# Attention by pairs of heads, in an order enforced on TensorE

## The chip, the cores and the metric

The kernel runs on one core of a Trainium2 chip. The metric is device time in microseconds (us) of one execution. TensorE (PE) multiplies, VectorE (DVE), ScalarE (ACT) and GpSimd (POOL) do the rest, SyncE (SP) issues the DMA transfers. PE's results go to PSUM, the other data to SBUF.

## The reference

Two transformer layers with adaptive norms (adaLN), for 512 tokens and 256 context tokens of width 1024, in float32. Three kinds of attention matter here; the rest (projections, SwiGLU feed-forward, norms, pooling) is outside the change.

```python
# layer 0: 12 query heads, 4 key/value heads, width 64; main queries see 768 keys, context queries 256
attn   = block_attention(q,  concat([kc, k]), concat([vc, v]), scale)
attn_c = block_attention(qc, kc, vc, scale)
# layer 1: 8 latent heads (key width 96, 768 keys) ...
o_mla  = block_attention(mq, concat([mkc, mk]), concat([mvc, mv]), mla_scale)
# ... and 8 neighbourhood heads: a window of the grid with a bias, and the 256 context keys
s = concat([s_win * scale + bias, s_ctx * scale]); p = softmax(s)
o_na = p[window] @ v_w + p[ctx] @ v_ctx
# block_attention: s = q k^T * scale; p = softmax(s); o = p v
```

## The kernel before

The two layers run one after the other: input norm and projection, attention, output projection (`mix_out`), feed-forward. Activations lie with channels in partitions and tokens in columns. Matmuls of float32 data are made of two or three passes: a value is split into a high and a low part of type fp32r (`QH`, `QL`; `KA` and its low part `LA`), and `mm3` (L143 to L145) or the pairs L786/L787, L813/L814, L1084/L1085 add them up.

Attention works on units. In layer 0 a unit is one head (of a pair of heads, `hd` 0 or 1) and one tile of 128 queries: 6 pairs x 4 tiles x 2 heads (`main_units`), then the context queries with 6 pairs x 2 tiles, both heads in one unit (`ctx_units`). In layer 1 come the neighbourhood units (`na_units`: 4 pairs x 4 blocks, both heads in a unit, 512 keys) and later the latent units (`mla_units`: 4 pairs x 4 tiles x 2 heads). A unit has three steps:

- `scores`: queries x keys on PE into PSUM, then `softmax` (L374 to L387): the maximum on DVE (L378), a small multiply (L380), the exponential with its sum on ACT (L383), the reciprocal on DVE (L385), the scaling on POOL (L387).
- `turn`: the 128 x 128 tiles of the probabilities are transposed on PE (`transposed`, L394) in blocks of three or four into one bank of PSUM, and a block is copied to SBUF (tile `PT`) by ACT (L173) or DVE (L175) in turn.
- the products of values: `V` x `PT`, 64 output channels of a head. The two heads of a pair write partitions 0 to 63 and 64 to 127 of one PSUM tile (L766, L1053, L1235). They are float32, and the trace shows two rows for each.

`pipeline` sets the order of these in the program: scores of unit i, a little background work, then the transposes of unit i - lag (lag 3, 2 and 2 units: `LAG`). The products are background too: `turn` of a pair's second head puts its products into the queue `pvq` in small steps (two key tiles, both heads), and each unit takes 1.4 to 1.8 steps out of it. The other background is `adaq` in layer 0 (16 steps of 8 matmuls of 32 output columns for adaLN weights, L213, each with its DMA loads, and two finishing steps) and `moreq` in latent attention (keys and values of the last four heads, with their transposes, L1129). Only the background has a fixed place (`tc.issue_after(s_().ins)`); else the scheduler of the framework orders each engine's instructions by its own simulated times, and engines run their own list in order.

## Time and profile before

| | us |
|---|---|
| median of three runs (lowest, highest) | 1768.34 (1766.82, 1770.72) |
| the profiled execution, and its span | 1769.58, 1767.8 |
| attention of layer 0, main queries (window 177 to 331): PE busy | 151.83 of 154 |
| neighbourhood attention (1115 to 1184): PE busy | 64.43 of 69 |
| latent attention (1226 to 1346): PE busy | 117.67 of 120 |

A row of the view in order of time is a run of equal instructions on one engine: start, busy time, engine, line, operation, what is written and read, shape, count, and in brackets the idle time before it and who ended it. A matmul's busy time reaches into the next one's, because matmuls are pipelined: from start to start is what a row costs. A row of the view of groups has the busy time in total and the mean of one, then idle time before it.

### The profile page before, as it was taken

What the parts mean: (1) busy time and instruction counts of PE and PEld (TensorE: products, weight loads), DVE (VectorE), ACT (ScalarE), POOL (GpSimd) and SP (SyncE); (2) the same over time, 40 slices, a digit from 0 to 9 for tenths busy, and PEclk for the clock granted to TensorE, in tenths of its full rate; (3) what the DMA queues carried; (4) which work ended last, traced back from release to release, by engine and by line L of the source; (5) the groups of instructions that cost most, each with busy time, mean ns of one, the idle gap of its engine ahead of it and who ended that gap; (6) DMA issues with size and microseconds to landing.
All of it is one profiled execution on the core that took longest, in us unless ns stands there. A gap on an engine that the chain in (4) does not pass through costs nothing.

```text
span 1767.8 us, 29063 instructions
## 1 busy us (share of the span) xinstructions
PE 1702.0 (96%) x11590; PEld 1489.2 (84%) x11590; DVE 946.7 (54%) x2072; ACT 634.5 (36%) x1237; POOL 252.8 (14%) x440
## 2 busy tenths in 40 slices
PE   6898999999999999999999999797999999999999
PEld 3687677788888888888889999677878999899897
DVE  5687565556855534533326875558756543333332
ACT  4454444635221221221124543445545332232231
POOL 1341333302000000000000202455321100000000
PEclk9899999999999999999999999898999999999999
DMA  7401323321534423522122222502003032222221
GB/s 270 159 34 52 119 96 133 130 96 49 187 126 151 169 77 115 175 86 71 61 72 85 84 76 60 127 19 70 30 19 132 13 120 96 96 96 96 95 76 57
DMA packets 60662, 171.23 MB, mean 97 GB/s; under 512 B 7152, under 2 KB 14576, under 8 KB 60528
## 3 DMA queue, kind: packets, MB, share of 16 engines
q1 hardware_dynamic: 60528, 169.39, 28.6%
q8 instruction: 91, 1.49, 0.3%
q14 instruction: 43, 0.35, 0.1%
HBM read 160.05 MB, written 4.19 MB: 93 GB/s over the span
## 4 chain that ended last, share of the span: by engine, by line
PE 92%; DVE 4%; ACT 1%; DMA 1%; issue 1%; SPq 0%; POOL 0%; ACTq 0%; DVEq 0%
PE ps_one L144 17%; PE ps_one L143 17%; PE ps_one L145 17%; PE ps_tp L394 5%; PE ps_tp L145 5%; PE ps_tp L143 5%; PE ps_tp L144 5%; PE ps_pv L766 3%; PE ps_pv L1235 2%; PE ps_big L143 2%; PE ps_big L144 2%; PE ps_big L145 2%; PE ps_pv L1053 1%; PE ps_pv L143 1%; PE ps_pv L144 1%; PE ps_pv L145 1%
## 5 line engine op out<-in xcount | busy, mean ns | idle before, releaser
L131 ACT CAST wH<-wraw 128x1024 fp32r<-128x1024 f32 (+5 forms) x209 | 194.3, 937 | 384.4 <-PE ps_one L144 188.3
L132 DVE TENSOR_TENSOR wL<-wraw,wH 128x1024 fp32r<-128x1024 f32 (+4 forms) x199 | 222.9, 1124 | 167.6 <-ACT wH L131 165.1
L145 PE MATMUL ps_one<-hH,wL 128*128 128x512 f32 (+1 forms) x704 | 236.8, 336 | 0.0
L144 PE MATMUL ps_one<-hL,wH 128*128 128x512 f32 (+1 forms) x704 | 236.8, 336 | 0.0
L143 PE MATMUL ps_one<-hH,wH 128*128 128x512 f32 (+1 forms) x704 | 236.8, 336 | 0.0
L145 PE MATMUL ps_tp<-hH,wL 128*128 128x256 f32 x704 | 196.6, 280 | 0.0
L144 PE MATMUL ps_tp<-hL,wH 128*128 128x256 f32 x704 | 196.3, 280 | 0.0
L143 PE MATMUL ps_tp<-hH,wH 128*128 128x256 f32 x704 | 196.1, 280 | 0.0
L145 PE MATMUL ps_one<-aH,wL 128*128 128x512 f32 (+1 forms) x560 | 194.1, 347 | 0.0
L144 PE MATMUL ps_one<-aL,wH 128*128 128x512 f32 (+1 forms) x560 | 194.0, 347 | 0.0
L143 PE MATMUL ps_one<-aH,wH 128*128 128x512 f32 (+1 forms) x560 | 193.5, 347 | 0.0
L297 POOL TENSOR_SCALAR hH<-nt 128x256 fp32r<-128x256 f32 (+1 forms) x72 | 39.5, 556 | 743.4 <-ACT nt L296 741.4
L145 PEld LDWEIGHTS ps_one<-hH,wL 128*128 128x128 f32 x704 | 132.3, 188 | 15.4
L144 PEld LDWEIGHTS ps_one<-hL,wH 128*128 128x128 f32 x704 | 132.3, 188 | 14.4
L143 PEld LDWEIGHTS ps_one<-hH,wH 128*128 128x128 f32 x704 | 132.3, 188 | 14.1
L387 POOL TENSOR_SCALAR prob<-prob,rs 128x768 f32<-128x768 f32 (+2 forms) x136 | 105.9, 782 | 229.6 <-DVE rs L385 89.1
L143 PEld LDWEIGHTS ps_tp<-hH,wH 128*128 128x128 f32 x704 | 132.4, 189 | 0.9
L144 PEld LDWEIGHTS ps_tp<-hL,wH 128*128 128x128 f32 x704 | 132.1, 188 | 1.0
L145 PEld LDWEIGHTS ps_tp<-hH,wL 128*128 128x128 f32 x704 | 132.3, 188 | 0.1
L143 PEld LDWEIGHTS ps_one<-aH,wH 128*128 128x128 f32 x560 | 105.8, 189 | 14.6
L144 PEld LDWEIGHTS ps_one<-aL,wH 128*128 128x128 f32 x560 | 105.7, 189 | 14.5
L145 PEld LDWEIGHTS ps_one<-aH,wL 128*128 128x128 f32 x560 | 105.6, 189 | 14.5
(300 smaller groups left out, 3567.0 us busy)
## 6 DMA issues: line engine op xcount, KB each, us to landing
wraw<-in_ada_dram SPq DMA_DIRECT2D x80, 512.0 KB, 3.9
wraw<-in_wg_dram SPq DMA_DIRECT2D x44, 512.0 KB, 3.6
wraw<-in_wu_dram SPq DMA_DIRECT2D x44, 512.0 KB, 3.5
wraw<-in_wd_dram SPq DMA_DIRECT2D x32, 384.0 KB, 3.0
wraw<-in_wd_dram SPq DMA_DIRECT2D x16, 512.0 KB, 3.5
wraw<-in_w1n_dram SPq DMA_DIRECT2D x12, 512.0 KB, 3.5
adaw<-in_adaq_dram SPq DMA_DIRECT2D x16, 256.0 KB, 5.4
wraw<-in_adaq_dram SPq DMA_DIRECT2D x8, 512.0 KB, 5.9
```

The source lines that it names most:

```text
L131: act.copy(H, raw[:, :cols])
L132: eng.tensor_tensor(L, raw[:, :cols], H.bitcast(F32), op=ALU.subtract)
L143: pe.matmul(o, aH, bH, start=first, stop=False)
L144: pe.matmul(o, aH, bL, start=False, stop=False)
L145: return pe.matmul(o, aL, bH, start=False, stop=last)
L297: last = (pool.tensor_scalar(H, t[:, :n], 1.0, 1.0, op0=ALU.mult, op1=ALU.mult), sub(L, t[:, :n], H))
L387: pool.tensor_scalar(pr[i], pr[i], r[:, i:i + 1], 1.0, op0=ALU.mult, op1=ALU.mult)
L394: pe.transpose(tp[:, 128 * i:128 * i + 128], b, ident)
L766: pe.matmul(st["pv"][64 * hd:64 * hd + 64, tq], V[kt][:, 64 * kv:64 * kv + 64], pts[hd][:, kt - k0, :], start=kt == k0, stop=kt == 5)
L1053: pe.matmul(o, v[:, hc], pts[hd][:, 2 * (1 - i) + j, :], start=i == 0 and j == 0, stop=i == 1 and j == 1)
L1235: pe.matmul(st["pv"][64 * hd:64 * hd + 64, tq], mV[kt][:, 64 * h:64 * h + 64], pts[hd][:, kt, :], start=kt == 0, stop=kt == 5)
```

## The change

`pipeline` is replaced by `paired`. A unit is now a pair of heads and a query tile (in the context part a pair and both tiles), and the order on PE is fixed: scores of pair i, the first two blocks of transposes of pair i-1, all products of pair i-2, one dose of background, the remaining blocks of transposes of pair i-1. Every block is tied to the last PE instruction issued before it (`Products` remembers it, `block` uses it). Products of the two heads alternate key tile by key tile. The transposes of a layer-0 or latent pair come in three blocks of four tiles (before: two blocks of three for each head), into one `PT` tile of twelve. The background rates are given per pair: `adaq` 0.8 (was 0.35 per unit), `moreq` 1.6 (was 0.8 per unit). Through `Products`, every PE row of the changed kernel carries L45 (matmul) or L49 (transpose).

```diff
-MPVR = 1.4
-PVR0 = 1.4
-PT0 = 6
-WS1, NAPT, MLPT = 4, 6, 5
-LAG = 3, 2, 2
+WS1, NAPT = 4, 6
+class Products:
+    def __init__(self, engine):
+        self.engine, self.last = engine, None
+    def matmul(self, *a, **kw):
+        self.last = self.engine.matmul(*a, **kw)
+        return self.last
+    def transpose(self, *a, **kw):
+        self.last = self.engine.transpose(*a, **kw)
+        return self.last
-    act, dve, pool, pe, sp = nc.scalar, nc.vector, nc.gpsimd, nc.tensor, nc.sync
+    act, dve, pool, pe, sp = nc.scalar, nc.vector, nc.gpsimd, Products(nc.tensor), nc.sync
-    def pipeline(units, fill, lag):
-        pend = []
+    def paired(units, fill):
         debt = [0.0] * len(fill)
+        def block(f):
+            with tc.issue_after(pe.last.ins):
+                f()
         def background():
             for i, (q, rate) in enumerate(fill):
                 debt[i] += rate
                 while debt[i] >= 1.0 and q:
                     debt[i] -= 1.0
-                    q.pop(0)()
+                    block(q.pop(0))
                 if not q:
                     debt[i] = min(debt[i], 1.0)
-        for s_, t_ in units:
-            with tc.issue_after(s_().ins):
-                background()
-            pend.append(t_)
-            if len(pend) > lag:
-                pend.pop(0)()
-        for t_ in pend:
+        units = iter(units)
+        turned = valued = None
+        while True:
+            unit = next(units, None)
+            if unit is None and turned is None and valued is None:
+                break
+            if unit:
+                block(unit[0])
+            for f in turned[1][:2] if turned else ():
+                block(f)
+            if valued:
+                block(valued[2])
             background()
-            t_()
+            for f in turned[1][2:] if turned else ():
+                block(f)
+            unit, turned, valued = None, unit, turned
-        def pv_steps(p, t, last, k0, pts, st, m):
...
+        def values_of(p, t, last, k0, pt, st, m):
             tq = slice(128 * t, 128 * t + 128)
-            def step(k1):
...
+            if t == 0:
+                st["pv"] = ps_pv([P, 512])
+            for kt in range(k0, 6):
                 for hd in range(2):
                     kv = p // 3 + 2 * hd
-                    for kt in (k1, k1 + 1):
-                        pe.matmul(st["pv"][64 * hd:64 * hd + 64, tq], V[kt][:, 64 * kv:64 * kv + 64], pts[hd][:, kt - k0, :],
-                                  start=kt == k0, stop=kt == 5)
...
+                    pe.matmul(st["pv"][64 * hd:64 * hd + 64, tq], V[kt][:, 64 * kv:64 * kv + 64], pt[:, hd, kt - k0, :],
+                              start=kt == k0, stop=kt == 5)
+            if t == last:
+                put_pair(st["pv"], 128 * last + 128, m)
         def main_units(p):
...
+                def turn(i, st=st):
+                    if i == 0:
+                        st["t"] = ap.tile([P, 12, 128], F32, tag="PT", name="PT", bufs=2)
+                    transposed([st["p"][j // 6][:, 0, 128 * (j % 6):128 * (j % 6) + 128] for j in range(4 * i, 4 * i + 4)],
+                               st["t"][:, 4 * i:4 * i + 4, :])
+                def values(t=t, st=st):
+                    values_of(p, t, 3, 0, st["t"].rearrange("p (h k) q -> p h k q", h=2), pvs, mixs[0][2 + p])
+                yield scores, [lambda i=i, turn=turn: turn(i) for i in range(3)], values
...
-        pipeline(all_units(), [(pvq, PVR0), (adaq, 0.35)], LAG[0])
-        for f in adaq + pvq:
+        paired(all_units(), [(adaq, 0.8)])
+        for f in adaq:
             f()
...
-        pipeline((u for pr in range(4) for u in na_units(pr)), [(pvq, 1.8)], LAG[1])
+        paired((u for pr in range(4) for u in na_units(pr)), [])
...
-        pipeline((u for pr in range(4) for u in mla_units(pr)), [(pvq, MPVR), (moreq, MKR)], LAG[2])
+        paired((u for pr in range(4) for u in mla_units(pr)), [(moreq, 2 * MKR)])
```

The neighbourhood, latent and context units are rewritten in the same manner; there the buffers of `prob` become 5 (as before), 4 (was 3) and 4 (as before), and the low queries of the neighbourhood part move to a memory pool of their own (`atq`).

The order that results on PE, in three places. First, layer 0's main queries; KA, QA belong to the first head of a pair, KB, QB to the second, LA and LBm, LBc are the low parts of the keys, and the numbers tell tiles apart. Before:

```order
L766 MATMUL ps_pv_1954<-PT_1902,V4_129 64x128
L766 MATMUL ps_pv_1954<-PT_1902,V5_130 64x128
L766 MATMUL ps_pv_1954<-PT_1928,V4_129 64x128
L766 MATMUL ps_pv_1954<-PT_1928,V5_130 64x128
L786 MATMUL ps_big_2012<-KB0_346,QB_651 128x512
L787 MATMUL ps_big_2012<-LBm_1815,QB_651 128x512
L786 MATMUL ps_big_2012<-KB0_346,QB_651 128x256
L787 MATMUL ps_big_2012<-LBc_1816,QB_651 128x256
L394 MATMUL ps_tp_2002<-ident_76,prob_1892 128x128 x3
L766 MATMUL ps_pv_1954<-PT_1971,V0_125 64x128
L766 MATMUL ps_pv_1954<-PT_1971,V1_126 64x128
L394 MATMUL ps_tp_2007<-ident_76,prob_1892 128x128 x3
```

After:

```order
L49 MATMUL ps_tp_2093<-ident_76,prob_1991 128x128 x4
L49 MATMUL ps_tp_2099<-ident_76,prob_1991 128x128 x2
L49 MATMUL ps_tp_2099<-ident_76,prob_1992 128x128 x2
L45 MATMUL ps_pv_1964<-PT_2021,V0_125 64x128 x2
L45 MATMUL ps_pv_1964<-PT_2021,V1_126 64x128 x2
L45 MATMUL ps_pv_1964<-PT_2021,V2_127 64x128 x2
L45 MATMUL ps_pv_1964<-PT_2021,V3_128 64x128 x2
L45 MATMUL ps_pv_1964<-PT_2021,V4_129 64x128 x2
L45 MATMUL ps_pv_1964<-PT_2021,V5_130 64x128 x2
L45 MATMUL ps_pv_1906<-wraw_2117,cs_112 32x512 x2
L45 MATMUL ps_pv_1906<-wraw_2119,cs_112 32x512 x2
L49 MATMUL ps_tp_2125<-ident_76,prob_1992 128x128 x4
```

Before, one score block of a head stands between two small blocks of products, and two key tiles of one head stand between transposes. After, both heads' scores, eight transposes and twelve products (two trace rows each) follow each other, the heads in alternation; one background step (the two rows of wraw) and the last four transposes close the iteration.

Second, neighbourhood attention, the same engine. Before:

```order
L394 MATMUL ps_tp_11801<-ident_76,prob_11606 128x128 x4
L1053 MATMUL ps_pv_11702<-PT_11707,mV4_9272 64x128
L1053 MATMUL ps_pv_11702<-PT_11707,mV5_9273 64x128
L394 MATMUL ps_tp_11807<-ident_76,prob_11607 128x128 x4
L1053 MATMUL ps_pv_11702<-PT_11708,mV4_9272 64x128
L1053 MATMUL ps_pv_11702<-PT_11708,mV5_9273 64x128
L1053 MATMUL ps_pv_11702<-PT_11707,V20_11021 64x128
L1053 MATMUL ps_pv_11702<-PT_11707,V21_11022 64x128
L1053 MATMUL ps_pv_11702<-PT_11708,V20_11021 64x128
L1053 MATMUL ps_pv_11702<-PT_11708,V21_11022 64x128
```

After:

```order
L49 MATMUL ps_tp_11093<-ident_76,prob_11009 128x128 x4
L49 MATMUL ps_tp_11099<-ident_76,prob_11010 128x128 x4
L45 MATMUL ps_pv_11105<-PT_11043,mV4_9194 64x128
L45 MATMUL ps_pv_11105<-PT_11044,mV4_9194 64x128
L45 MATMUL ps_pv_11105<-PT_11043,mV5_9195 64x128
L45 MATMUL ps_pv_11105<-PT_11044,mV5_9195 64x128
L45 MATMUL ps_pv_11105<-PT_11043,mV0_9190 64x128
L45 MATMUL ps_pv_11105<-PT_11044,mV0_9190 64x128
L45 MATMUL ps_pv_11105<-PT_11043,mV1_9191 64x128
L45 MATMUL ps_pv_11105<-PT_11044,mV1_9191 64x128
L45 MATMUL ps_one_11116<-nKA_9228,nQH0_9220 128x256
```

The products of the unit two back, which stood in pieces between transposes, are one piece behind both blocks of transposes of the unit one back.

Third, the start of latent attention on PE; qr are query tiles with their norms, mKH and mQH the high parts of keys and queries. Before:

```order
L1129 MATMUL ps_tp_12478<-ident_76,qr_12375 96x128 x4
L1129 MATMUL ps_tp_12491<-ident_76,qr_12375 96x128 x4
L143 MATMUL ps_big_12701<-mKH_12075,mQH_12067 128x512
L144 MATMUL ps_big_12701<-mKL_12076,mQH_12067 128x512
L145 MATMUL ps_big_12701<-mKH_12075,mQL_12068 128x512
L143 MATMUL ps_big_12701<-mKH_12075,mQH_12067 128x256
L144 MATMUL ps_big_12701<-mKL_12076,mQH_12067 128x256
L145 MATMUL ps_big_12701<-mKH_12075,mQL_12068 128x256
L1129 MATMUL ps_tp_12619<-ident_76,qr_12540 96x128
L1129 MATMUL ps_tp_12632<-ident_76,qr_12540 96x128
L1129 MATMUL ps_tp_12619<-ident_76,qr_12540 96x128 x3
L1129 MATMUL ps_tp_12632<-ident_76,qr_12540 96x128 x3
```

After:

```order
L49 MATMUL ps_tp_12404<-ident_76,qr_12301 96x128 x4
L49 MATMUL ps_tp_12417<-ident_76,qr_12301 96x128 x4
L49 MATMUL ps_tp_12545<-ident_76,qr_12466 96x128
L49 MATMUL ps_tp_12558<-ident_76,qr_12466 96x128
L49 MATMUL ps_tp_12545<-ident_76,qr_12466 96x128 x3
L49 MATMUL ps_tp_12558<-ident_76,qr_12466 96x128 x3
L49 MATMUL ps_tp_12573<-ident_76,qr_12516 96x128
L49 MATMUL ps_tp_12586<-ident_76,qr_12516 96x128
L49 MATMUL ps_tp_12573<-ident_76,qr_12516 96x128 x3
L49 MATMUL ps_tp_12586<-ident_76,qr_12516 96x128 x3
L45 MATMUL ps_big_12629<-mKH_12001,mQH_11993 128x512
L45 MATMUL ps_big_12629<-mKL_12002,mQH_11993 128x512
```

The first scores stood ahead of the transposes of the last query tiles, and now stand behind all of them.

## Rows read from the trace of the kernel before

**Rows 1.** Stages: window, length, then busy us of each engine, PEclk, DMA.

```profile
177.00:331.00 154.00, 151.83 (x1241) 108.26 (x1242) 93.14 (x239) 80.16 (x187) 49.54 (x62) 0.98 0.37 134
...
1115.00:1184.00 69.00, 64.43 (x524) 52.95 (x524) 41.81 (x178) 39.00 (x94) 34.15 (x73) 0.94 0.26 67
1226.00:1346.00 120.00, 117.67 (x890) 94.10 (x890) 76.13 (x206) 58.78 (x130) 34.74 (x48) 0.98 0.06 19
```

**Rows 2.** The values products alone (L766, L1053, L1235): busy us and count.

```profile
177.00:331.00 154.00, 52.60 (x576) 35.95 (x576) 0.98 0.37 134
...
1115.00:1184.00 69.00, 27.45 (x256) 19.25 (x256) 0.94 0.26 67
...
1226.00:1346.00 120.00, 40.44 (x384) 27.12 (x384) 0.98 0.06 19
```

**Rows 3.** PE in time, 243 to 250 us: start, us, line, operands, count.

```profile
243.07 0.66 PE L766 MATMUL ps_pv<-PT,V 128*64 128x128 f32 x8
...
244.29 0.47 PE L786 MATMUL ps_big<-KA,QA 128*128 128x512 f32 x1
...
244.84 0.28 PE L786 MATMUL ps_big<-KA,QA 128*128 128x256 f32 x1
244.96 0.28 PE L787 MATMUL ps_big<-LA,QA 128*128 128x256 f32 x1
245.17 0.65 PE L766 MATMUL ps_pv<-PT,V 128*64 128x128 f32 x4
...
248.00 1.15 PE L766 MATMUL ps_pv<-PT,V 128*64 128x128 f32 x16
249.07 0.87 PE L394 MATMUL ps_tp<-ident,prob 128*128 128x128 f32 x6
249.70 0.47 PE L786 MATMUL ps_big<-KA,QA 128*128 128x512 f32 x1
```

**Rows 4.** PE in time: third pair, context attention, its last values.

```profile
184.04 0.48 PE L786 MATMUL ps_big<-KA,QA 128*128 128x512 f32 x1
...
312.25 0.39 PE L813 MATMUL ps_big<-KA,QA 128*128 128x256 f32 x1 [0.35 <-ACT prob L383]
...
312.92 1.06 PE L213 MATMUL ps_pv<-wraw,cs 128*32 128x512 f32 x8
...
341.08 0.48 PE L143 MATMUL ps_one<-mp,wH 128*128 128x512 f32 x1
...
350.90 0.66 PE L766 MATMUL ps_pv<-PTc,V 128*64 128x128 f32 x8
```

**Rows 5.** First layer, 200 to 300 us, by form: busy us, mean ns of one.

```profile
L378 DVE TENSOR_REDUCE mx<-ps_big 128x1 f32<-128x768 f32 x34 | 32.5, 956 | 26.3 <-PE ps_big L787 25.8
...
L383 ACT ACTIVATE prob<-ps_big,nb 128x768 f32<-128x768 f32 x34 | 30.8, 906 | 1.6 <-DVE nb L380 1.6
L387 POOL TENSOR_SCALAR prob<-prob,rs 128x768 f32<-128x768 f32 x34 | 30.8, 905 | 71.2 <-DVE nb L380 35.3 <-DVE rs L385 20.5 <-PE ps_tp L394 13.7
...
L173 ACT COPY PT<-ps_tp 128x384 f32<-128x384 f32 x34 | 16.3, 479 | 49.9 <-PE ps_tp L394 49.9
```

**Rows 6.** Context attention, 331 to 351 us, by form.

```profile
L383 ACT ACTIVATE prob<-ps_big,nb 128x256 f32<-128x256 f32 x9 | 4.2, 471 | 0.7 <-PE ps_big L814 0.7
```

**Rows 7.** Neighbourhood attention, 1122 to 1183 us, by form.

```profile
L387 POOL TENSOR_SCALAR prob<-prob,rs 128x512 f32<-128x512 f32 x32 | 22.3, 702 | 30.4 <-DVE nb L380 19.4 <-DVE rs L385 10.1
L383 ACT ACTIVATE prob<-ps_one,nb 128x512 f32<-128x512 f32 x32 | 22.0, 690 | 13.8 <-issue 4.9 <-POOL mKH L1132 2.6 <-PE ps_tp L394 2.1
```

**Rows 8.** PE in time at the start of neighbourhood attention.

```profile
1122.92 0.58 PE L1084 MATMUL ps_one<-nKA,nQH 128*128 128x256 f32 x1 [3.91 <-ACT prob L383]
1123.30 0.41 PE L1085 MATMUL ps_one<-nKA,nQL 128*128 128x256 f32 x1
```

**Rows 9.** PE in time, latent attention: first scores, last values.

```profile
1225.90 0.77 PE L143 MATMUL ps_big<-mKH,mQH 128*128 128x512 f32 x1 [4.36 <-DVE qr L1156]
...
1343.59 1.56 PE L1235 MATMUL ps_pv<-PT,mV 128*64 128x128 f32 x20
```

More of the change, by code (lines that the diff above doesn't have):

```diff
@@ L804, in ctx_units, with scores @@
             kp = p // 3
-            for t in range(2):
-                tq = slice(TM + 128 * t, TM + 128 * t + 128)
-                st = {}
-                def scores(tq=tq, st=st):
+            st = {}
+            def scores():
+                st["p"] = []
+                for t in range(2):
+                    tq = slice(TM + 128 * t, TM + 128 * t + 128)
                     S = ps_big([P, 2, 512])
@@ L1022, in trunk @@
     mixs = [None] * 8
-    pvq = []
-    with tc.tile_pool(name="at1", bufs=1, side="left") as ap:
+    with tc.tile_pool(name="atq", bufs=1, side="left") as aq, tc.tile_pool(name="at1", bufs=1, side="left") as ap:
         def low_queries(pr):
-            QB = [ap.tile([P, TM], F32R, tag="nQB" + x, name="nQB" + x, bufs=2) for x in "HL"]
+            QB = [aq.tile([P, TM], F32R, tag="nQB" + x, name="nQB" + x, bufs=2) for x in "HL"]
             for a, b in zip(QQ[pr], QB):
@@ L1251, in mla_units, with scores @@
             for t in range(4):
-                pts = []
-                for hd in range(2):
-                    tq = slice(128 * t, 128 * t + 128)
-                    (QH, QL), (KH, KL_) = mQ[2 * pr + hd], mK[2 * pr + hd]
-                    st = {}
-                    def scores(QH=QH, QL=QL, KH=KH, KL_=KL_, tq=tq, hd=hd, st=st):
+                tq = slice(128 * t, 128 * t + 128)
+                st = {}
+                def scores(tq=tq, st=st):
+                    st["p"] = [ap.tile([P, 1, TT], F32, tag="P", name="prob", bufs=4) for _ in range(2)]
+                    for hd in range(2):
+                        (QH, QL), (KH, KL_) = mQ[2 * pr + hd], mK[2 * pr + hd]
@@ L1274, in mla_units, with turn @@
-                    yield scores, turn
-        pipeline((u for pr in range(4) for u in mla_units(pr)), [(pvq, MPVR), (moreq, MKR)], LAG[2])
-        for f in pvq:
-            f()
+                            mm3(S[:, ko], (QH[:, tq], QL[:, tq]), (KH[:, ko], KL_[:, ko]), True, True)
+                        softmax(S[:, :TT].unsqueeze(1), 1, TT, 96 ** -0.5, [st["p"][hd][:, 0, :]])
+                def turn(i, st=st):
+                    if i == 0:
+                        st["t"] = ap.tile([P, 12, 128], F32, tag="PT", name="PT", bufs=2)
+                    transposed([st["p"][j // 6][:, 0, 128 * (j % 6):128 * (j % 6) + 128] for j in range(4 * i, 4 * i + 4)],
+                               st["t"][:, 4 * i:4 * i + 4, :])
@@ new lines, in values @@
+                def values(t=t, tq=tq, st=st):
+                    if t == 0:
+                        pvs["pv"] = ps_pv([P, 512])
+                    for kt in range(6):
+                        for hd in range(2):
+                            h = 2 * pr + hd
+                            pe.matmul(pvs["pv"][64 * hd:64 * hd + 64, tq], mV[kt][:, 64 * h:64 * h + 64],
+                                      st["t"][:, 6 * hd + kt, :], start=kt == 0, stop=kt == 5)
+                    if t == 3:
+                        mixs[pr] = group_pair(0, "mix")
+                        put_pair(pvs["pv"], 512, mixs[pr])
@@ L1279, in trunk @@
+                yield scores, [lambda i=i, turn=turn: turn(i) for i in range(3)], values
+        paired((u for pr in range(4) for u in mla_units(pr)), [(moreq, 2 * MKR)])
     gm.close()
```

117 lines of the change are left out of this document (35 added, 82 removed).

## The prediction

> **What bounds the kernel now.** I read the page's first part, then the windows of the attention stages, then TensorE (PE) in order of time, then the groups of the other engines. PE is busy nearly throughout, in the first layer's attention 151.83 of 154 us, beside 93 of VectorE (DVE), 80 of ScalarE (ACT) and 50 of GpSimd (POOL) [rows 1]. So time falls there only if PE gets less to do, or does the same work quicker. In the neighbourhood stage PE still has 64.43 of 69 us, but the first wait there is 3.91 us on a softmax [rows 1, 8].
>
> The quick and slow ways of the same work stand side by side. A products block of 8 with both heads lasts 0.66 us; one of 4, all of one head, 0.65; one of 16, 1.15 [rows 3]. Busy times reach some 0.08 us into what follows (the 16 start at 248.00, the next block at 249.07: 1.07). So 8 take about 0.58 to the next start and 16 take 1.07: 0.061 each, plus 0.09 for the block. The 4 of one head cost 0.145 each. Two heads write different halves of the array's columns (`[64 * hd:64 * hd + 64]`) and overlap; one head alone does not. Entering costs too: the 256-column score matmul ahead of a block starts 0.21 us before the block, the one ahead of that 0.12 [rows 3]. I count 0.09 for an entry.
>
> **The change, part by part.** *First layer, main queries.* 576 products rows are busy 52.60 us [rows 2] in 69 blocks (counted in the same view of 177 to 331 us); less 0.08 overlap for each, 47.1 us. After: 24 blocks of 24, each 0.09 + 24 x 0.061 = 1.56, together 37.4. Saved: 9.7, and 45 entries at 0.09, 4.1. Transposes become fewer, larger blocks; their number stays.
>
> The same from the other end, by the iteration. Scores of two heads: the first 0.55 for its two 512-column matmuls (244.29 to 244.84) and 0.24 for the other two, the second head a little less (no block change ahead): 1.51. Six transposes take 0.63 (249.07 to 249.70) [rows 3], so the first two blocks of four 0.84, the third 0.42. Products 1.56 and entry 0.09. Sum: 4.43 us. A background step of the adaLN weights lasts 1.06, 0.99 without overlap [rows 4]; 15 of them lie in the stretch. Before, the third pair's scores start at 184.04 and those of the first context unit at 312.25 [rows 4], 22 pairs later: 128.2 us. After: 22 x 4.43 + 15 x 0.99 + 1 for the two finishing steps = 113.3, so the context starts at 297.4, 14.9 earlier. That is 1.1 above the sum over blocks, about what the 0.35 wait of [rows 4] and others like it make. The background steps load their weights through SP, at 0.8 a pair instead of 0.35 a head: the same transfers, slightly sooner, on DMA engines that are 0.37 busy here [rows 1]. I cost that at nothing; were one late, the third transposes block and everything behind it would wait, since nothing may pass it any more.
>
> *The wait that the order adds.* Behind a transposes block that waits, the products, the background and the next scores now wait too. So a pair's probabilities must be there when their turn comes, one iteration later. The chain for the second head, from the start of its iteration: scores 1.5; both maxima 0.96 each on DVE (the first starts at 0.8), the small multiply and a PSUM copy between; then two exponentials of 0.91 on ACT behind up to two copies; then POOL's 0.91 [rows 5]. Without copies in the way it is ready at about 0.8 + 2 x 0.96 + 0.3 + 0.91 + 0.2 (readout of the sum) + 0.3 (reciprocal and hand-overs, my estimate) + 0.91 = 5.3; with one 0.48 ACT copy, grown to 0.6 for 512 columns, and a DVE copy of 0.6 in the way, 6.5. It is needed in the second transposes block, at 4.43 + 1.51 + 0.42 + 0.1 = 6.5. It fits, barely. I put 2 us on such waits; the bound below is 0, the one above 24 x 0.4 = 9.6 (all copies in the way, both on ACT). Copies get fewer (three for twelve blocks instead of four), which only helps engines that are idle half the time.
>
> *First layer, context.* 30 us lie between 312.25 and the effective end before: the last products start at 350.90 and take 0.6, and 39 matmuls of the output projection (first at 341.08, 0.233 apart) were done by then, so 351.5 - 9.1 = 342.4 [rows 4]. After, one unit is a whole pair with both query tiles: 8 score matmuls, 8 transposes, 16 products, 1.1 + 0.84 + 1.16 = 3.1 on PE. ACT needs four exponentials of 0.47 with their readouts (0.2) and a copy of 0.6, 3.3 [rows 6], and the chain through them is about 5.2 long, needed 1.5 into the next iteration: 3.7. So 4.1 for the first (it carries the main queries' products), 4 x 3.8, then the last pair's scores 1.1, chain 4.0, transposes 0.84, products 1.1 with nothing beside them: 26.4. End at 297.4 + 2 + 26.4 = 325.8. Gain of the layer: 342.4 - 325.8 = 16.6.
>
> *Neighbourhood attention.* On PE 34 blocks of products, 27.45 us [rows 2], become 16 of 16 at 1.07: 27.45 - 34 x 0.08 - 17.1 + 18 x 0.09 = 9.3 saved. But here the softmax decides. The engines' work of a unit is 41.81 / 16 = 2.6 on DVE, 2.4 on ACT, 2.1 on POOL [rows 1], and one unit's chain is scores 1.0, DVE's part for two heads 2.4, the second exponential 0.69 and readout 0.2, POOL 0.70 [rows 7], 0.2 hand-over: 5.2. Before, transposes follow their scores by two units, so this is covered; after, by one, and the second head's transposes come about 1.5 into the next iteration. So an iteration lasts 3.7, against 3.05 of PE work and about 3.6 now. Sixteen of them with the same filling and draining: 1.6 later than now, less the shorter last products. I take 1 us lost; the bounds are 9 gained (PE decides after all) and 9 lost (4.2 an iteration, copies ahead of exponentials).
>
> *Latent attention.* 384 rows, 40.44 us [rows 2] in 55 blocks: 36.0 without overlap. After, 16 x 1.56 = 25.0; entries 39 x 0.09 = 3.5. Saved 14.5. An iteration has 2.13 of scores, 1.27 of transposes and 1.65 of products, 5.1, longer than the chain's need, and the background of keys and values fills the first eight as before, so no waits inside; the 2.3 us in which PE is idle between 1226 and 1346 now [rows 1] go, I take 2. Against it: the transposes of the last query tiles now all stand ahead of the first scores, which begin at 1225.90 today, after 4.36 us of waiting for such a tile [rows 9]; the last tile comes later, so the first scores do. I put 2 us on it, with 0 and 6 as bounds: what stood between first and second scores is done by then. And the last pair's transposes and products have nothing beside them, some 3 us more than the 20 products at 1343.59 that end it now [rows 9]. 14.5 + 2 - 2 - 3 = 11.5.
>
> **Sum.** 16.6 - 1 + 11.5 = 27.1. The profiled execution took 1769.58, its span 1767.8, so 1742.5; against the median of the runs shown, 1768.34, 1741.2. I say 1743.
>
> **The rivals.**
> *(a) The order makes latency the bound.* First-layer iterations at 4.8 (24 x 0.37 = 9), neighbourhood at 4.2 (8 more), context 2: 27 - 19 = 8 gained, 1760; half of it, 1751. For it: the sum of 6.5 against 6.5 above, and the second exponential behind copies. Against: DVE is 0.6 and ACT 0.5 busy [rows 1].
> *(b) All copies go ahead of the exponentials, in all stages.* Then the chain of a first-layer pair is ready at 7.6, the iteration is 5.5, and latent attention, with scores of 2.13, goes to 5.6: 24 x 1.07 + 16 x 0.5 = 34 lost, with neighbourhood 8: 1743 + 42 = 1785, slower. It decides from about 0.65 us of wait in each of the 40 long iterations. Against: the copies wait for PE's transposes, and maxima are asked for earlier than that.
> *(c) The clock falls.* After a wait of 3.91 us the 256-column score matmuls are 0.41 busy, later ones 0.28 [rows 8, 3]: the granted clock is at its lower level, 1.2 GHz. If the 0.65 us in each neighbourhood iteration did that, its 3.05 us on PE became 5.3, 16 x 1.6 = 26 lost: about 1769, no change. Against: after the 0.35 us wait at 312.25 nothing slows down (the window's clock is 0.98) [rows 4, 1].
> The Trainium skill (TensorE: Matmul & The Clock Gate, HAM oscillation — how this bites in real kernels) describes a kernel in which a wait on every turn of its loop throttles TensorE again, so that each turn starts slowly. Applied to the wait in each neighbourhood iteration it gives (c), 1769 instead of 1743; the 0.35 us wait, after which nothing slowed, speaks for 1743.
> *(d) PE decides everywhere.* Neighbourhood gains 9 and no first-layer wait appears: 1743 - 12 = 1731.
>
> **Chances.** Forecast (1737 to 1750) 0.57, (a) 0.22, (b) 0.07, (c) 0.03, (d) 0.11. The measurement tells 0.2%, 3.5 us, from no change; a (a) with twice its price ends there. Faster 0.87, same 0.05, slower 0.08. The range reaches from (d) into (a): 1730 to 1759.
>
> **What would show it.** Right: L45 rows of 24 products lasting 1.6 and starting 4.4 apart in the first layer; context scores near 297; no wait for ACT copies or POOL's probabilities over 0.3 us there; neighbourhood iterations of 3.7 with one wait on POOL in each; latent iterations of 5.1 after the background is gone. Wrong: products that still take 0.09 each (the heads do not overlap), transposes waiting about 1 us in each first-layer iteration, or PEclk below 0.9 in an attention stage.

## The result, and the profile after

The changed kernel takes 1740.28 us (median; 1739.45 to 1743.03), the kernel before 1769.5 (1766.82 to 1770.72). The ratio is 0.984, its interval 0.9822 to 0.9857: about 25 to 31 us faster. The forecast was 1743.

Each matmul of the one trace has its counterpart in the other, so the gain can be put to stages. Between the same rows of the two profiled executions (spans 1767.8 and 1737.7, difference 30.1):

| stretch | forecast | measured |
|---|---|---|
| ahead of the first attention | 0 | 1.4 |
| first layer's attention | 16.6 | 17.6 |
| between, feed-forward and projections | 0 | 1.5 |
| neighbourhood attention | -1 | -1.5 |
| latent attention to the output projection | 11.5 | 11.1 |

The 1.4 and 1.5 are no work of the change. The 1.4 is there by 30 us, ahead of all that the edit touches, and its cause stays open. For the 1.5 the waits are the same in both traces (1.7, 0.9 and 0.8 us, near 970 us before and 951 after), but behind them the granted clock of TensorE was 0.94 from 960 to 990 us before, and 1.00 from 941 to 971 in the changed kernel: some rows ran at the lower level in the one execution and none in the other. Below, stages that an experiment left alone differ by up to 3.3 us for such reasons.

TensorE in order of time in the changed kernel, answering to [rows 3]: start, busy time, line, operands, count.

```profile
246.72 1.03 PE L49 MATMUL ps_tp<-ident,prob 128*128 128x128 f32 x8
247.69 1.53 PE L45 MATMUL ps_pv<-PT,V 128*64 128x128 f32 x24
249.15 1.07 PE L45 MATMUL ps_pv<-wraw,cs 128*32 128x512 f32 x8
250.15 0.66 PE L49 MATMUL ps_tp<-ident,prob 128*128 128x128 f32 x4
250.56 0.48 PE L45 MATMUL ps_big<-KA,QA 128*128 128x512 f32 x1
...
254.89 0.48 PE L45 MATMUL ps_big<-KA,QA 128*128 128x512 f32 x1
```

24 rows of products take 1.46 us to the next start (247.69 to 249.15); 1.56 was reckoned. An iteration lasts 4.33 us (250.56 to 254.89), 5.3 with a background step; 4.43 and 5.42 were reckoned.

The products by groups, answering to [rows 2]: first the first layer's main queries from 177 to 297 us (22 of the 24 blocks), then latent attention (busy us, mean ns of one). A block's rows are 1.53 and 1.55 busy; the 384 rows of latent attention, 40.44 before, are down by 15.6.

```profile
L45 PE MATMUL ps_pv<-PT,V 128*64 128x128 f32 x528 | 33.7, 277 | 0.0
```

```profile
L45 PE MATMUL ps_pv<-PT,mV 128*64 128x128 f32 x384 | 24.8, 277 | 0.0
```

TensorE in order of time at the places of [rows 4], then its waits from 177 to 330 us (who, for whom: us in total, times, longest).

```profile
183.52 0.48 PE L45 MATMUL ps_big<-KA,QA 128*128 128x512 f32 x1
...
296.64 0.36 PE L45 MATMUL ps_big<-KA,QA 128*128 128x256 f32 x1
...
321.91 0.73 PE L45 MATMUL ps_one<-mp,wH 128*128 128x512 f32 x2
...
331.41 0.66 PE L45 MATMUL ps_pv<-PTc,V 128*64 128x128 f32 x8
```

```profile
PE ps_big L45 <- ACT prob L395: 6.3, 6, 4.5
PE ps_tp L49 <- POOL prob L399: 0.5, 2, 0.4
```

The context starts at 296.64 (297.4 was said), 15.6 earlier than before. The 4.5 us stand at the second pair's scores, as they did before. What is left is one wait of 0.7 us for a free score buffer in the main part, and in the context units 1.2 for free score buffers and 0.5 for probabilities. The output projection (from 321.91) fills the end of the context stage, which the forecast had left empty.

In neighbourhood attention the picture is another. TensorE's waits from 1085 to 1165 us, a piece of its rows, one row of VectorE (a reciprocal that a scaling needs), and GpSimd's rows of the same time:

```profile
PE ps_tp L49 <- POOL prob L399: 17.5, 14, 4.3
```

```profile
1098.10 0.56 PE L45 MATMUL ps_one<-nKA,nQH 128*128 128x256 f32 x1
...
1119.69 1.09 PE L45 MATMUL ps_pv<-PT,mV 128*64 128x128 f32 x16
1120.71 0.39 PE L45 MATMUL ps_one<-nKA,nQH 128*128 128x256 f32 x1
...
1124.72 1.92 PE L49 MATMUL ps_tp<-ident,prob 128*128 128x128 f32 x8 [2.80 <-POOL prob L399]
1126.58 1.12 PE L45 MATMUL ps_pv<-PT,mV 128*64 128x128 f32 x8
...
1128.39 0.39 PE L45 MATMUL ps_one<-nKA,nQH 128*128 128x256 f32 x1
...
1155.63 0.39 PE L45 MATMUL ps_one<-nKA,nQH 128*128 128x256 f32 x1
```

```profile
1121.83 0.15 DVE L397 RECIPROCAL rs<-sm 128x1 f32<-128x1 f32 x1
```

```profile
1121.25 0.40 POOL L1074 TENSOR_SCALAR bias<-bias 128x256 f32<-128x256 f32 x1 [2.20 <-DMA bias<-in_bias_dram]
1121.71 0.81 POOL L1143 MEMSET mKL<- 32x256 f32 x3
1122.61 0.40 POOL L1074 TENSOR_SCALAR bias<-bias 128x256 f32<-128x256 f32 x1
1123.07 0.81 POOL L1143 MEMSET mKH<- 32x256 f32 x3
1123.98 2.69 POOL L399 TENSOR_SCALAR prob<-prob,rs 128x512 f32<-128x512 f32 x4
```

Bias tiles of coming units, and memory fills for latent attention, stand in GpSimd's list ahead of the probabilities. The reciprocal is there at 1121.98, the scaling (L399) starts at 1123.98; the first bias tile ahead of it had itself waited 2.20 us for its load. The transposes wait, and behind them, in the enforced order, all else. Followed through the trace in this way, eight of the 13 waits after the first, 10.3 of their 13.2 us, end with scalings that GpSimd began 0.9 to 2.0 us after their reciprocals, right behind a bias tile or a fill; at the other five it began within 0.2 us. The transposes and products after the 2.80 us also run at the clock's lower level (16 products 1.81 us, 1126.58 to 1128.39, instead of 1.02).

Iterations last 4.43 us on average (third to last unit's scores: 1098.10 to 1155.63, 13 of them), not 3.7. That costs some 10 us more than forecast, yet the stage came out as forecast. What paid for it is not in the prediction at all. SyncE's loads of the low queries and the first neighbourhood scores on TensorE, first of the kernel before, then of the changed one:

```profile
1109.98 1.10 SPq L370 DMA_DIRECT2D nQBH<-nQH  x2
...
1115.21 0.55 PE L1084 MATMUL ps_one<-nKA,nQH 128*128 128x256 f32 x1 [5.29 <-DMA nQH<-nQH]
```

```profile
1066.97 1.11 SPq L382 DMA_DIRECT2D nQBH<-nQH  x2
...
1089.18 0.28 PE L45 MATMUL ps_one<-nKA,nQH 128*128 128x256 f32 x1
```

Before, the low queries were loaded when the projections had ended, and the first neighbourhood scores waited 5.29 us for DMA (at 1115.21). In the changed kernel they are loaded 22 us ahead of those scores (1089.18), and nothing waits.

### The profile page after: what moved, and what is told of

The parts are those of the page before. It is cut to its first block, busy times and chain, and to the rows that moved or that the text cites. A ratio compares the mean times of both kernels' runs of the same rounds, so it can differ in the third digit from the quotient of the medians.

```text
span 1737.7 us, 28925 instructions
## 1 busy us (share of the span) xinstructions
PE 1655.2 (95%) x11590; PEld 1469.8 (85%) x11590; DVE 942.6 (54%) x2052; ACT 631.0 (36%) x1217; POOL 251.8 (14%) x440
## 4 chain that ended last, share of the span: by engine, by line
PE 87%; DVE 6%; ACT 3%; POOL 2%; DMA 1%; issue 1%; SPq 0%; POOLq 0%; ACTq 0%; DVEq 0%
PE ps_one L45 52%; PE ps_tp L45 15%; PE ps_pv L45 9%; PE ps_big L45 7%; PE ps_tp L49 5%; ACT prob L395 1%; POOL prob L399 1%; DVE mx L390 0%; DVE wL L144 0%; DVE win L648 0%; DVE ss L350 0%; ACT wH L143 0%; DVE rq L269 0%; DVE qn L598 0%; DVE nwt L267 0%
## 5 line engine op out<-in xcount | busy, mean ns | idle before, releaser
L45 PE MATMUL ps_one<-hH,wL 128*128 128x512 f32 (+1 forms) x704 | 236.8, 336 | 0.0
L45 PE MATMUL ps_one<-hL,wH 128*128 128x512 f32 (+1 forms) x704 | 236.7, 336 | 0.0
L45 PE MATMUL ps_one<-hH,wH 128*128 128x512 f32 (+1 forms) x704 | 236.7, 336 | 0.0
L45 PE MATMUL ps_tp<-hH,wL 128*128 128x256 f32 x704 | 196.6, 280 | 0.0
L45 PE MATMUL ps_tp<-hL,wH 128*128 128x256 f32 x704 | 196.3, 279 | 0.0
L45 PE MATMUL ps_tp<-hH,wH 128*128 128x256 f32 x704 | 196.0, 280 | 0.0
L45 PE MATMUL ps_one<-aH,wL 128*128 128x512 f32 (+1 forms) x560 | 194.0, 347 | 0.0
L45 PE MATMUL ps_one<-aL,wH 128*128 128x512 f32 (+1 forms) x560 | 193.9, 347 | 0.0
L45 PE MATMUL ps_one<-aH,wH 128*128 128x512 f32 (+1 forms) x560 | 193.5, 347 | 0.0
L45 PEld LDWEIGHTS ps_one<-hH,wL 128*128 128x128 f32 x704 | 132.2, 188 | 15.4
L45 PEld LDWEIGHTS ps_one<-hL,wH 128*128 128x128 f32 x704 | 132.2, 188 | 14.4
L45 PEld LDWEIGHTS ps_one<-hH,wH 128*128 128x128 f32 x704 | 132.3, 188 | 14.2
L399 POOL TENSOR_SCALAR prob<-prob,rs 128x768 f32<-128x768 f32 (+2 forms) x136 | 105.2, 782 | 195.7 <-DVE rs L397 157.0
L45 PEld LDWEIGHTS ps_tp<-hH,wH 128*128 128x128 f32 x704 | 132.3, 188 | 0.9
L45 PEld LDWEIGHTS ps_tp<-hL,wH 128*128 128x128 f32 x704 | 132.0, 188 | 1.0
L45 PEld LDWEIGHTS ps_tp<-hH,wL 128*128 128x128 f32 x704 | 132.2, 188 | 0.1
L49 PE MATMUL ps_tp<-ident,prob 128*128 128x128 f32 x656 | 99.5, 285 | 20.6 <-POOL prob L399 18.0
L45 PEld LDWEIGHTS ps_one<-aH,wH 128*128 128x128 f32 x560 | 105.8, 189 | 14.7
L45 PEld LDWEIGHTS ps_one<-aL,wH 128*128 128x128 f32 x560 | 105.6, 189 | 14.5
```

What stands on the lines that cost most here:

```text
L45: self.last = self.engine.matmul(*a, **kw)
L49: self.last = self.engine.transpose(*a, **kw)
L399: pool.tensor_scalar(pr[i], pr[i], r[:, i:i + 1], 1.0, op0=ALU.mult, op1=ALU.mult)
```

## The experiments

Twelve runs, each against the kernel before on the same chip. The table puts each profiled execution to stages, as difference in us to the changed kernel's (plus: longer); the neighbourhood column reaches into the projections behind that stage (to 1183.8 us in the changed kernel), and the time ahead of the first layer and between it and the neighbourhood stage is left out.

| run | median us | first layer | neighbourhood | latent |
|---|---|---|---|---|
| kernel before | 1767 to 1770 | +17.6 | -1.5 | +11.1 |
| heads apart | 1777.18 | +17.9 | +6.8 | +11.6 |
| free order | 1753.49 | +16.8 | -11.8 | +7.5 |
| two visits | 1749.67 | +3.9 | +2.1 | +1.8 |
| neighbourhood lag 2 | 1726.00 | -0.4 | -15.2 | +1.5 |
| alternation alone | 1759.88 | +13.9 | -2.3 | +7.0 |
| lag 2, loose start | 1723.14 | -0.1 | -15.6 | -3.3 |
| blocks of three | 1742.89 | +2.3 | -3.3 | +1.9 |
| first layer lag 2 too | 1731.17 | +1.6 | -14.3 | -0.7 |
| products first | 1735.46 | -0.3 | -3.7 | -1.4 |
| lag 2, loose start, again | 1719.44 | -1.9 | -17.2 | -4.2 |
| queries in the old pool | 1748.79 | -2.4 | +10.6 | +0.1 |
| before, new pool | 1759.48 | +15.4 | -9.5 | +11.4 |

**Heads apart.**

```diff
-            for kt in range(k0, 6):
-                for hd in range(2):
+            for hd in range(2):
+                for kt in range(k0, 6):
```

(and the same in the two other stages)

> The changed kernel with one thing undone: in every block of products all key tiles of the first head come first, then all of the second, instead of the two heads in alternation. Number of blocks, order and instructions are the same. Theory (the alternation makes the two column halves work side by side): a block of 24 goes from 1.46 us (rows of the changed kernel, start to start) to about 24 x 0.109 + 0.1 = 2.7, so 24 x 1.25 = 30 us in the first layer, 4 in its context, 16 x 1.25 = 20 in latent attention, and up to 12 in neighbourhood attention, less what its waits cover: 55 to 62 us slower, 1795 to 1803, slower than the kernel before. Rival (only the number of blocks counts, which is 24 for 69 in the first layer): within 2 us of 1740.

1777.18 us, ratio to before 1.0051 (1.0036 to 1.0066). The alternation is needed, for without it the changed kernel is slower than the one before; but 37 us, not 55 to 62. Two blocks of its trace:

```profile
249.29 2.46 PE L45 MATMUL ps_pv<-PT,V 128*64 128x128 f32 x24
251.68 1.06 PE L45 MATMUL ps_pv<-wraw,cs 128*32 128x512 f32 x8
...
325.31 1.15 PE L45 MATMUL ps_pv<-PTc,V 128*64 128x128 f32 x16
```

24 rows take 2.39 us, 0.93 more than in alternation, not 1.25. And the context's 16, four of one head and then four of the other by turns, are 1.15 busy against 1.09 in the changed kernel. TensorE starts the second head's products while four rows of the first still stand ahead of them, but not twelve: in the block of 24 only eight rows in its middle (249.21 to 249.60) start 0.05 apart, four of each head, the others 0.11. With that reach the blocks of 8 of the kernel before overlapped already [rows 3].

**Free order.**

```diff
         def block(f):
-            with tc.issue_after(pe.last.ins):
-                f()
+            f()
```

> The changed kernel without the tie of each block to the last TensorE instruction: the program is written in the same order, alternation and larger transpose blocks stay, but the scheduler places the instructions by its own simulated times. Theory (long undivided blocks need the enforced order): the scheduler cuts products into two or three pieces a pair and puts single heads' scores between, which loses 0.2 to 0.3 us for each extra piece, some 50 of them, so 10 to 15 us of the 29 gained: 1750 to 1756. Rival A (the order itself does nothing, alternation is all): 1738 to 1742. Rival B (the forced order costs waits that a free one avoids): below 1737, by shorter neighbourhood and context stages.

1753.49, ratio 0.9914 (0.9899 to 0.9929): the theory's figure, but by two effects of opposite sign, the second of them that of rival B. In the first layer nearly the whole gain is lost (16.8 of 17.6), in latent attention 7.5 of 11.1; the program has 141 blocks of products on TensorE instead of 61, and its rows show why (start, busy time):

```profile
249.69 0.66 PE L45 MATMUL ps_pv<-PT,V 128*64 128x128 f32 x8
250.28 1.05 PE L45 MATMUL ps_pv<-wraw,cs 128*32 128x512 f32 x4
251.27 0.66 PE L49 MATMUL ps_tp<-ident,prob 128*128 128x128 f32 x4
251.85 1.07 PE L45 MATMUL ps_pv<-wraw,cs 128*32 128x512 f32 x8
252.85 0.66 PE L49 MATMUL ps_tp<-ident,prob 128*128 128x128 f32 x4
```

Background steps too are cut: 4 rows, two groups of 32 columns, cost 0.99 (250.28 to 251.27), as much as the 8 of all four groups (251.85 to 252.85). In neighbourhood attention, though, the free order is 11.8 us faster than the enforced one.

**Two visits.**

```diff
-            for f in turned[1][:2] if turned else ():
+            parts = valued[2] if valued else ()
+            for f in turned[1][:1] if turned else ():
                 block(f)
-            if valued:
-                block(valued[2])
+            for f in parts[:1] if len(parts) > 1 else ():
+                block(f)
+            for f in turned[1][1:2] if turned else ():
+                block(f)
+            for f in parts[-1:]:
+                block(f)
```

> The changed kernel with the products of a pair in the first layer's main queries and in latent attention cut into two blocks of 12, one behind the first and one behind the second block of transposes; heads alternate as before, nothing else changes. Theory (each visit of the products costs about 0.09 for entering and 0.09 for the block, maybe 0.05 more for leaving): 40 more visits at 0.18 to 0.25: 7 to 10 us slower, 1747 to 1750. Rival (visits are free and the gain is all alternation): 1740, within 1.5 us.

(`parts` are the products of key tiles 0 to 2 and of 3 to 5; `values` and the units are cut to match.) 1749.67 (1747.03 to 1753.86), ratio 0.9902 (0.988 to 0.9924): visits are not free. Pieces of two iterations:

```profile
243.65 0.66 PE L49 MATMUL ps_tp<-ident,prob 128*128 128x128 f32 x4
244.23 0.88 PE L45 MATMUL ps_pv<-PT,V 128*64 128x128 f32 x12
245.04 1.06 PE L45 MATMUL ps_pv<-wraw,cs 128*32 128x512 f32 x8
...
247.93 0.60 PE L49 MATMUL ps_tp<-ident,prob 128*128 128x128 f32 x4
248.46 0.88 PE L45 MATMUL ps_pv<-PT,V 128*64 128x128 f32 x12
```

A block of 12 rows lasts 0.81 to the next start, two of them 1.62 against 1.46 for one of 24. The eight transposes that the visit cuts last 0.53 and 0.58, against 0.97 in one block (246.72 to 247.69 in the changed kernel). So one more visit costs 0.30 us, 0.16 of it in the products, more than the theory's 0.18 to 0.25. It shows in the iterations of latent attention without background (5.32 against 5.03), and from the third pair's scores to the first of the context units (119.5 us against 113.1, 0.29 for each of 22 pairs). The first layer's +3.9 in the table is less than 24 x 0.30, because the first two pairs were 2.7 us shorter in this execution, by a wait and by the clock.

**Neighbourhood attention at a lag of two.**

```diff
-        paired((u for pr in range(4) for u in na_units(pr)), [])
+        paired((u for pr in range(4) for u in na_units(pr)), [], lag=2)
-                    st["p"] = [... name="prob", bufs=5) ...]
+                    st["p"] = [... name="prob", bufs=7) ...]
```

> The changed kernel with neighbourhood attention alone at a lag of two: scores of pair i, transposes of pair i-2, products of pair i-3, with 7 buffers for probabilities instead of 5. Theory (there the enforced lag of one makes the softmax chain the bound; the trace shows 14 waits for scaled probabilities, 17.5 us in all, 4.35 of them at the start): the waits but the first go, 8 to 12 us faster, 1728 to 1732. Rival (VectorE, ScalarE and GpSimd with the bias and memory fills set the pace of that stage whatever the lag): less than 3 us faster, 1737 or more.

1726.0 (1723.41 to 1727.03), ratio 0.9758 (0.9744 to 0.9773): 15.2 us out of that stage, more than the theory's 8 to 12. Of these 11.3 are waits (6.2 us in all instead of 17.5); with them goes the stretch at the lower clock behind the 2.80 us wait, and the rest was not taken apart. TensorE's waits from 1085 to 1150 us, and one iteration:

```profile
PE ps_one L45 <- ACT prob L395: 3.3, 1, 3.3
PE ps_tp L49 <- POOL prob L399: 2.9, 3, 1.6
```

```profile
1114.46 0.39 PE L45 MATMUL ps_one<-nKA,nQH 128*128 128x256 f32 x1
...
1116.48 1.10 PE L45 MATMUL ps_pv<-PT,mV 128*64 128x128 f32 x16
1117.50 0.39 PE L45 MATMUL ps_one<-nKA,nQH 128*128 128x256 f32 x1
```

An iteration without waits is now 3.04 us (1114.46 to 1117.50), TensorE's own work; the forecast's 3.05 for it was right. With the waits that are left it is 3.46 on average (13 from 1095.77 to 1140.70).

**Alternation alone,** in the kernel before:

```diff
-                for hd in range(2):
-                    kv = p // 3 + 2 * hd
-                    for kt in (k1, k1 + 1):
+                for kt in (k1, k1 + 1):
+                    for hd in range(2):
+                        kv = p // 3 + 2 * hd
```

> The kernel before with one thing done: inside each small step of products the two heads alternate key tile by key tile; queues, rates, units and the free order stay. The program then has 166 blocks of products on TensorE where the kernel before has 168 and the changed one 61. Theory (overlap needs both heads in one block, and every block costs some 0.2 us): the scheduler now starts 48 blocks with one lone product, so lone products get only somewhat fewer; 0 to 6 us faster than before, 1762 to 1768. Rival (alternation alone is the gain): 15 us or more faster, below 1753.

1759.88 (1759.62 to 1760.08), ratio 0.9952 (0.9937 to 0.9966): 8.7 us, more than the theory's 0 to 6 and far from the rival's 15. Of the 17.6 us of the first layer it gives 3.7, of the 11.1 of latent attention 4.1. The rest needs the blocks.

**Lag of two, loose start of latent attention.** In `paired` the first unit's scores are issued without the tie (`loose=1`).

> The run with neighbourhood attention at a lag of two, and in latent attention the scores of the first unit not tied to what stands ahead of them, so that they stand ahead of the last query tiles' transposes, as in the kernel before. Theory (the tie made TensorE wait at the start of latent attention: 2.80, 2.74 and 1.76 us ahead of transposes of query tiles in the changed kernel): the first scores fill one of these waits: 2 to 5 us faster than that run, 1721 to 1724. Rival (the second pair's scores are what counts, and they wait for the last query tile anyway): within 1 us of 1726.

1723.14 (1719.3 to 1723.39), ratio 0.9739 (0.9724 to 0.9753). The start of latent attention, first in the changed kernel, then here:

```profile
1204.45 1.05 PE L49 MATMUL ps_tp<-ident,qr 128*96 128x128 f32 x8 [2.80 <-DVE mQL L362]
1208.24 2.17 PE L49 MATMUL ps_tp<-ident,qr 128*96 128x128 f32 x8 [2.74 <-DVE nwt L268]
1212.17 2.13 PE L49 MATMUL ps_tp<-ident,qr 128*96 128x128 f32 x8 [1.76 <-DVE mQL L362]
1213.94 0.78 PE L45 MATMUL ps_big<-mKH,mQH 128*128 128x512 f32 x1
```

```profile
1193.59 0.77 PE L45 MATMUL ps_big<-mKH,mQH 128*128 128x512 f32 x1 [4.56 <-DVE qr L1172]
...
1195.64 1.91 PE L49 MATMUL ps_tp<-ident,qr 128*96 128x128 f32 x8
```

The scores stand ahead of the last query tiles again. The stage is 4.8 us shorter than in the run it builds on (-3.3 and +1.5 in the table), 3.3 shorter than in the changed kernel: the size of the theory, though the medians of the two runs are no more than 2.9 apart.

**Blocks of three.** `range(4 * i, 4 * i + 4)` becomes `range(3 * i, 3 * i + 3)`, with four blocks a pair.

> The changed kernel with transposes in blocks of three tiles again (four blocks and four PSUM copies a pair in the first layer's main queries and latent attention; two blocks ahead of the products, two behind the background). Theory (fewer, larger copies save work only on engines that are not the bound): within 2 us of the changed kernel, 1739 to 1742. Rival (the 40 copies saved are part of the gain): 4 us slower or more, 1744 up.

1742.89, but the runs are 1739.44, 1739.61, 1746.16 and 1747.68; ratio 0.9858 (0.9834 to 0.9881). Two runs speak for either side, and the run with two visits has the same two groups (1747, and 1752 to 1754) in one kernel, so the spread can't be put to the blocks. The profiled execution's span equals the changed kernel's within 0.2 us, but only because neighbourhood attention, which the edit leaves alone, is 3.3 us shorter in it; the two stages with the edit are 2.3 and 1.9 longer. In the first layer 1.2 us of that are two waits for VectorE at the background's finishing steps. What the larger blocks are worth stays open, at 0 to some 6 us.

**First layer at a lag of two** (on top of the neighbourhood's; 6 probability buffers):

> The run with neighbourhood attention at a lag of two, and the first layer's attention at a lag of two as well, with 6 buffers of probabilities instead of 4. Theory (its main queries are bound by TensorE: only 0.5 us of waits for probabilities are in the changed kernel's trace; the context units have 1.7 us of waits): 0 to 2 us faster than that run, 1724 to 1726. Rival (the softmax chain holds the first layer's iterations up, as the forecast's 6.5 against 6.5 left open): 5 us faster or more, 1721 or less.

1731.17, ratio 0.9789 (0.9772 to 0.9805): 5 us slower than the run it builds on, neither the theory nor the rival. In the profiled execution the first layer is 2.0 us longer than there. TensorE waits 2.01 us at 292.30 for ScalarE's copy of the last background result (`adat`, L230), and rows behind it run at the lower clock (0.97 from 285 to 335 us, against 1.00). Another 3.3 us lie between the stages, where the waits are the same within 0.3 us and the clock is not (0.89 from 942 to 972 us, against 1.00). The rival, 5 us or more faster, falls: the first layer's iterations are TensorE's.

**Products first.** In neighbourhood attention the products of unit i-2 stand ahead of the transposes of unit i-1:

```diff
+            if valued and first:
+                block(valued[2])
             for f in turned[1][:2] if turned else ():
                 block(f)
-            if valued:
+            if valued and not first:
                 block(valued[2])
```

> The changed kernel with one move in neighbourhood attention: the products of unit i-2 stand ahead of the transposes of unit i-1 instead of behind them. Lag, buffers and all other stages stay. The transposes get 1.07 us more time, and nothing else waits longer. Theory (there the softmax chain is a little too long for the order; the 13 waits after the first in the changed kernel's trace are 0.3 to 2.8 us, and about 7.5 us of their sum lies within the first 1.05 us of each unit): 6 to 9 us faster, 1731 to 1735. Rival (the waits come from GpSimd being held up for 2 to 4 us by memory fills and bias tiles that stand ahead of the probabilities in its list; 1 us does not cover that, and a shift only moves the wait): at most 3 us faster, 1737 or more.

```profile
PE ps_tp L49 <- POOL prob L399: 8.9, 7, 4.3
```

1735.46 (1732.5 to 1737.64), ratio 0.9808 (0.9791 to 0.9824), between the two. Waits for probabilities fall from 17.5 to 8.9 us, but the ends of the hold-ups remain (1.72 and 1.01 us still), and 2.0 us of new waits stand at the products, for the PSUM copies. At the end of the stage's own work 7.6 us are gained, what the theory said; in the projections behind it a new wait of 3.67 us, for a query tile from VectorE, takes back most of the rest to the table's -3.7.

**Lag of two and loose start again, beside it:**

> The fastest version so far again (neighbourhood attention at a lag of two, first scores of latent attention not tied), here beside the run with the products moved up. Theory (two units of lag cover the whole softmax chain with what GpSimd has ahead of it): 1719 to 1724, 8 us or more below the run with products moved up. Rival (products moved up do the same with fewer buffers): the two within 4 us once the 3 us of the untied first scores are taken off.

1719.44 (1718.26 to 1723.21), ratio 0.9724 (0.971 to 0.9739): 16 us below the run above, so moving the products does not replace the lag. The comparison holds the loose start too, 3 to 5 us of the 16. This version is the fastest: its two runs are 17 and 21 us below the changed kernel.

**The pool of the low queries,** undone in the changed kernel, and done alone in the one before (there the reverse diff):

```diff
-    with tc.tile_pool(name="atq", ...) as aq, tc.tile_pool(name="at1", ...) as ap:
+    with tc.tile_pool(name="at1", bufs=1, side="left") as ap:
-            QB = [aq.tile([P, TM], F32R, tag="nQB" + x, name="nQB" + x, bufs=2) for x in "HL"]
+            QB = [ap.tile([P, TM], F32R, tag="nQB" + x, name="nQB" + x, bufs=2) for x in "HL"]
```

> The changed kernel with the low queries of neighbourhood attention (nQB) back in the pool of the probabilities, as before; nothing else. In the kernel before, their loads are issued at 1109.98 us, and the first scores wait 5.29 us for them; in the changed one they are issued at 1066.97, 22 us sooner against the first scores, and nothing waits. Theory (the pool of its own frees the loads from what the other pool's memory still holds): the loads come late again, the first neighbourhood scores wait about 5 us, and the run is 3 to 6 us slower than the changed kernel, 1743 to 1746. Rival (the loads come sooner because the order before them changed): no wait, 1740 within 2 us.

> The kernel before with only the low queries of neighbourhood attention in a pool of their own. Theory (as for the run with the old pool): the 5.29 us wait at the first neighbourhood scores goes; the first exponentials start up to 5 us sooner and the free order passes that on: 3 to 6 us faster than before, 1762 to 1766. Rival (something else holds the softmax, so the wait moves to it): within 1.5 us of before.

Undone: 1748.79 (1747.74 to 1750.71), ratio 0.9892 (0.9873 to 0.9911). Done alone: 1759.48 (1758.93 to 1760.32), ratio 0.9953 (0.9938 to 0.9968). The waits of the first run, 1080 to 1175 us:

```profile
PE ps_tp L49 <- POOL prob L399: 17.6, 11, 5.0
PE ps_one L45 <- DMA nQH<-nQH: 5.3, 1, 5.3
```

Both theories hold in kind, and both were too small: the wait comes or goes, and stretches at the lower clock with it. Undone, the waits for probabilities are the same in sum (17.6 us), the wait for the load is 5.3 of the 10.6 us, and the granted clock is 0.85 from 1085 to 1175 us, against 0.94 in the changed kernel (1085 to 1165). By the table, the pool is worth 8.0 us in the old order (-1.5 to -9.5) and 10.6 in the new; the new order of neighbourhood attention costs 12.1 with the old pool and 9.5 with the new. The two edits cancel to 1.5.

## Why the prediction was right

*First layer (16.6 said, 17.6 measured).* The sum held step by step: block, iteration, start of the context. Of the 2 us set aside for waits on probabilities none came among the main queries, and 0.5 in the context units: the chain fits (the run with a lag of two gains nothing). The end is better than the 325.8 that were reckoned: the last products at 331.41 + 0.6, less 31 projection matmuls of 0.233 done by then, make 324.8. (Before, the trace has 33 of them ahead of the last products, where the prediction counted 39: the end was 343.8 rather than 342.4. The difference, 19.0, holds the 1.4 us that came ahead of the stage.)

*Which part of the work it is.* The forecast laid the gain to blocks and to overlap. Alternation alone gives 3.7 of 17.6; enforced order without alternation loses everything (+17.9); alternation and large blocks without the tie lose 16.8. So it is not a sum of parts: overlap and few visits both have to be there, and without the tie the scheduler cuts the blocks. The background's rate (0.8 a pair, where 0.35 a unit makes 0.7) was not tried alone.

*Latent attention (11.5 and 11.1).* Right in sum. The later start was priced at 2 us, and the loose start measures it at 3.3 to 4.8, one execution each; so the other terms, 13.5 together, gave 14.4 to 15.9. They were not measured one by one; an iteration after the background is 5.03 (1278.13 to 1283.16), where 5.1 was said.

*Neighbourhood attention (-1 and -1.5).* Right by chance. The step that failed is "an iteration lasts 3.7": it measured 4.43, and the order costs 9.5 to 12.1 us there, at or above the bound of 9. The forecast took the chain's length from sums of one unit's operations; GpSimd's list, in which fills and bias tiles of other work stand ahead of the probabilities, was not read. The step that was missing is the pool `atq`. The prediction calls the 3.91 us on a softmax the first wait of the stage; the first is the one of 5.29 us for the low queries, at 1115.21. It was not priced, and no term looked at what the pool's move does to the loads on SyncE. So two errors of 8 to 12 us had opposite signs.

*The rivals.* (a) came true in one of its three places, neighbourhood attention, and was paid for by the pool. (b) did not come: first-layer iterations last 4.33 us, not 5.5. (c) happened in part: in the changed kernel's neighbourhood stage rows ran at the lower level, 1.2 GHz, after the waits of 4.35 and 2.80 us, and not after the later ones of 1.76 us and less; in the run with products first they did after one of 1.72. By the Trainium skill (TensorE: Matmul & The Clock Gate, HAM oscillation — how this bites in real kernels) a kernel that waits on every turn of its loop can start each turn slowly. Here stretches of slow rows begin at two of the 14 waits, and the granted clock from 1085 to 1165 us was 0.94. (d) is what the lag of two reaches: 1731 was said, 1726 measured.

## What to carry to other kernels

Where products of half the array's width alternate with full-width work, count visits and pairs from the trace, and write the order down if the scheduler cuts the blocks. Give an enforced order a lag that covers what stands in the list of each engine of the chain, not the sum of one unit's operations alone: here a lag of two did, a lag of one did not. Read those engines' own rows between two units. And price each small edit of a diff, memory pools too: here the place of a transfer's target decided when it started. And look at the granted clock before a difference of 1 to 3 us between two executions is put to an edit.

## What the runs showed of the hardware

- Two heads' products overlap although their instructions do not alternate: rows of four and four (context of the run with heads apart) cost 1.15 against 1.09 us busy, twelve and twelve 2.39 against 1.46 from start to start. So matmuls of the second column half started ahead of up to four rows of the first that stand before them in the program.
- Matmuls of 32 output columns: two of the four column groups alone cost as much as all four (0.99 and 1.00 us a step), so a background step that is cut in two pays twice.
- With the same waits of 1.7, 0.9 and 0.8 us in the same rows, the granted clock was 1.00 in the changed kernel (941 to 971 us) and 0.94 in the kernel before (960 to 990 us): 1.5 us between two executions, with no change of the work. What decides it is not shown.
